# Reordering the first microseconds of a float16 gated MLP: loads, turns, plain columns and one cast

## The chip, the cores and the metric

One Trainium2 chip (trn2), one core of it. The metric is the device time of the program in microseconds (us), the median of several executions. The span of a profile is 1.7 to 1.9 us shorter than that time. A run would count as slow if it were over 1.5% above the fastest of its kernel.

## The reference

```python
# x: (16, 256, 512)   w1: (512, 4096)   w2: (2048, 512), all float32
h = x @ w1
gate, value = np.split(h, 2, axis=-1)
h = np.maximum(gate, 0) * value
return (h @ w2).astype(np.float32)
```

## The kernel before

The kernel rounds to float16 and multiplies 2x2 blocked matrices with Strassen-like schemes of seven products (P1 to P7), so it needs sums and differences of blocks as operands. It works in four stages of 1024 rows each. In a stage, 16 "blocks" of 128 hidden columns give g (first product), and then g times w2 gives the output (second product). In the first stage the operands have to be made while TensorE already wants them: x comes in as float32 and is turned (transposed, 128 columns at a time) by TensorE; the four sums S1 to S4 of x come from VectorE; the four differences T1 to T4 of w1, for each pair of blocks, come from GpSimd; ScalarE casts the parts of w1 that need no difference. To have something to multiply before the sums exist, blocks 0 and 1 are done as "plain" products of eight matmuls per half of the rows. Products land in the tiles X, W and Y (in PSUM, the memory for results); an "eviction" is the instruction of VectorE or ScalarE that reads such a tile out, and the program lets TensorE write the tile again only after it.

```python
    # names of the profile: x_A, x_S = x and its sums; w_B, w_T = w1 and its differences;
    # v_B, v_T = the same of w2; w_stage = where w1 lands, later the sums of g
    fetch(0, nc.scalar)                 # w1 block 0, on ScalarE's queue
    fetch_first(0)                      # x blocks 0..3
    fetch(1, nc.sync)                   # w1 block 1
    make_identity(nc, ident)
    fetch_first(1)                      # x blocks 4..7
    fetch(2, nc.sync)                   # w1 blocks 2 and 3
    fetch(3, nc.sync)                   # w1 blocks 4 and 5
    # ... cut
    rest = plain_w(0)
    turn_first(xo, 0, 0, new_w())       # four float32 turns, two evictions
    keep_busy(2)                        # warm matmuls
    turn_first(xo, 0, 1, new_x())
    rest()
    keep_busy(4)
    turn_first(xo, 0, 2, new_x())
    keep_busy(2)
    turn_first(xo, 0, 3, new_w())
    keep_busy(2)
    plain[0].products(0, *first_half, half)     # gate and value together
    plain_w(1)()
    fetch(4, nc.sync)
    plain[0].products(0, *first_half, other)
    plain[0].value()                    # ScalarE: W out of PSUM
    plain[0].gate(0)                    # VectorE: max(X, 0) * v
    # ... cut: block 1 with the turns of x blocks 4..7 between, then the sums of x
    prepare(2)                          # GpSimd: T1..T4 of blocks 2 and 3, each for both blocks
    copy_some(3)                        # ScalarE: their three casts
    fetch(5, nc.sync)                   # w1 blocks 8 and 9, into the place of 2 and 3
    # ... cut
    prepare(3)

    # in a block of the first product
        def P1(self):
            # ... X <- B11 A11 ; then ScalarE copies X to Y
            nc.scalar.copy(out=self.Y, in_=self.X)

    # first stage, once: GpSimd, the differences of w2
                if (s, n, jb) == (0, "P7", 13):
                    nc.gpsimd.tensor_tensor(vop["T1"], vop["T3"], vop["B11"], op=SUB)
                    nc.gpsimd.tensor_tensor(vop["T2"], vop["B22"], vop["T1"], op=SUB)

    # second product: a "look" squares one operand on ScalarE (a range check), 1.05 us
        def P4(self):
            nc.scalar.activation(self.o[:, 1, :DO // 2], self.Y, COPY, scale=1 / GS)
            self.send(1, slice(0, DO // 2 if self.end else DO))
            if self.t < (2 if self.s else 3):
                some_look()
```

## Time and profile before

| | before |
|---|---|
| median time (first three runs: 310.92 to 311.54) | 311.07 us |
| span in the profile | 309.2 us |
| TensorE busy | 301.5 us (98%) |
| first plain product | 8.68 us |
| P1 of block 2 / P4 of block 2 | 17.39 / 23.30 us |
| last matmul | 304.27 us |

The page's head and its share of each engine:

```profile
span 309.2 us, 5211 instructions
PE 301.5 (98%) x1870; PEld 183.2 (59%) x1870; DVE 236.4 (76%) x378; ACT 177.0 (57%) x350; POOL 153.7 (50%) x186
```

TensorE (PE) is the limit. Whatever it gains must come from places where it waits or does work that counts for nothing, and those lie at the start. The next lines are from the timeline of PE before: start and length in us, engine, line, operation, output and inputs; in brackets the idle time before it and what ended it. One line merges several instructions.

```profile
1.27 3.17 PE L145 MATMUL Y<-warm 128*128 128x512 f16 x7 [1.27 <-DVE warm L141]
4.62 0.63 PE L448 MATMUL W<-ident,x_A 128*128 128x128 f32 x4 [0.18 <-DMA x_A<-in_x_dram]
...
8.68 0.38 PE L301 MATMUL X<-x_A,w_B 128*128 128x256 f16 x2
...
17.39 0.59 PE L233 MATMUL X<-x_A,w_B 128*128 128x512 f16 x2
17.82 0.59 PE L233 MATMUL W<-x_S,w_T 128*128 128x512 f16 x2
18.64 0.59 PE L233 MATMUL X<-x_A,w_B 128*128 128x512 f16 x2 [0.23 <-ACT Y L240]
...
23.30 0.59 PE L233 MATMUL Y<-x_A,w_T 128*128 128x512 f16 x2 [0.47 <-DVE cc L266]
```

The first product that is needed starts at 8.68 us. Block 2 starts at 17.39 us, and P4 of block 2, which needs the last of the differences, at 23.30 us. I use that P4 as a milestone: what comes before it is the start, what comes after is "the body". A pair of 512-column matmuls should follow the one before by 0.43 us, so the start 18.64 after 17.82 hides a stall of 0.39 us, more than the bracket shows, because the length of a matmul is modelled.

GpSimd (POOL) before: its first difference waits for w1 blocks 2 and 3 to land.

```profile
15.57 1.36 POOL L215 TENSOR_TENSOR w_T<-w_stage 128x512 f16<-128x512 f32 x1 [5.44 <-DMA w_stage<-in_w_dram]
...
54.48 1.53 POOL L187 DMA_DIRECT2D x<-in_x_dram  x3
56.01 4.09 POOL L580 TENSOR_TENSOR v_T<-v_T,v_B 128x2048 f16<-128x2048 f16 x1
60.18 4.06 POOL L581 TENSOR_TENSOR v_T<-v_B,v_T 128x2048 f16<-128x2048 f16 x1
```

VectorE (DVE) before, where the sums of g for the second product begin, in the same stretch:

```profile
64.02 0.78 DVE L164 TENSOR_TENSOR w_stage<-g 128x1024 f16<-128x1024 f16 x1
64.88 0.69 DVE L164 TENSOR_TENSOR w_stage<-w_stage,g 128x1024 f16<-128x1024 f16 x1
```

### The profile page before, as it was taken

The numbers are of one execution on the slowest core, as the hardware profiler recorded it, in microseconds if no ns is written. First come the engines' busy times: TensorE is split into PE (matmuls) and PEld (weight loads), VectorE is DVE, ScalarE is ACT, GpSimd is POOL, SyncE is SP. The second block draws the span as 40 slices with busy tenths as digits, with TensorE's granted clock in tenths as the row PEclk, the third lists the DMA queues.
The fourth block names the chain that finished last, engine by engine and source line by source line (L and its number), as shares of the span: only waits on it lengthen the run. The fifth ranks groups of instructions, "written<-read, shape, count | busy, mean of one in ns | idle before, by whom it ended". The sixth has DMA issues, their size and how long they took to land.

```text
span 309.2 us, 5211 instructions
## 1 busy us (share of the span) xinstructions
PE 301.5 (98%) x1870; PEld 183.2 (59%) x1870; DVE 236.4 (76%) x378; ACT 177.0 (57%) x350; POOL 153.7 (50%) x186
## 2 busy tenths in 40 slices
PE   7999999999999999999999999999999999999994
PEld 3844444588854444478864444458884444448883
DVE  1598888889678888887538888888536888888841
ACT  2588886445865555537855555546956555553231
POOL 2199999930048899500028889700006988700000
PEclk9999999999999999999999999999999999999999
DMA  7977696998594233001354400000325110000132
GB/s 236 355 230 251 176 232 87 196 214 149 164 303 101 69 70 68 2 0 47 127 184 105 119 0 4 0 0 15 122 103 171 37 34 1 0 3 0 70 136 72
DMA packets 37340, 32.87 MB, mean 106 GB/s; under 512 B 14400, under 2 KB 32320, under 8 KB 37184
## 3 DMA queue, kind: packets, MB, share of 16 engines
q1 hardware_dynamic: 31904, 25.70, 27.2%
q0 software_dynamic: 4352, 6.29, 11.8%
q10 hardware_dynamic: 1056, 0.52, 0.6%
q8 instruction: 15, 0.25, 0.3%
q14 instruction: 13, 0.11, 0.1%
HBM read 27.26 MB, written 12.58 MB: 129 GB/s over the span
## 4 chain that ended last, share of the span: by engine, by line
PE 93%; DVE 2%; DMA 2%; issue 1%; SPq 0%; ACT 0%; DVEq 0%
PE Y L233 26%; PE X L233 17%; PE W L233 17%; PE Y L333 14%; PE X L333 9%; PE W L333 9%; DMA x_A<-in_x_dram 2%; DVE x_S L164 1%; PE X L448 1%; DVE g L308 1%; PE X L301 1%; PE W L301 1%; PE W L448 0%; PE Y L150 0%; DVE x_S L450 0%
## 5 line engine op out<-in xcount | busy, mean ns | idle before, releaser
L233 PEld LDWEIGHTS <-w_T 128*128 128x128 f16 x496 | 48.5, 98 | 57.5 <-issue 1.0
L170 POOL TENSOR_TENSOR fold<-xh 128x1024 f32<-128x1024 f16 x16 | 30.3, 1894 | 93.1 <-DMA xh<-x 92.1
L233 PE MATMUL X<-x_A,w_B 128*128 128x512 f16 x248 | 73.7, 379 | 0.2 <-ACT Y L240 0.2
L233 PE MATMUL Y<-x_S,w_T 128*128 128x512 f16 x248 | 73.8, 379 | 0.0
L233 PEld LDWEIGHTS <-w_B 128*128 128x128 f16 x372 | 36.4, 98 | 42.6 <-issue 0.8
L240 ACT COPY Y<-X 128x512 f32<-128x512 f32 x62 | 35.4, 570 | 39.8 <-PE X L233 39.5
L260 DVE SCALAR_TENSOR_TENSOR cc<-W,pu 128x512 f32<-128x512 f32 x62 | 42.8, 691 | 19.5 <-ACT pu L254 19.5
L254 ACT ACTIVATE pu<-Y 128x512 f32<-128x512 f32 x62 | 37.0, 597 | 34.1 <-PE Y L233 32.8
L173 POOL TENSOR_TENSOR fold<-fold 128x512 f32<-128x512 f32 (+2 forms) x96 | 51.8, 540 | 7.5
L333 PEld LDWEIGHTS <-w_stage 128*128 128x128 f16 x512 | 50.0, 98 | 6.3 <-issue 0.4
L266 DVE SCALAR_TENSOR_TENSOR cc<-Y,pu 128x512 f32<-128x512 f32 x62 | 42.8, 691 | 7.2 <-PE Y L233 0.7
L261 DVE SCALAR_TENSOR_TENSOR g<-X,cc 128x512 f16<-128x512 f32 x62 | 42.9, 691 | 2.3
L276 DVE SCALAR_TENSOR_TENSOR g<-Y,cc 128x512 f16<-128x512 f32 x62 | 42.2, 681 | 1.8 <-PE Y L233 1.8
L333 PEld LDWEIGHTS <-g 128*128 128x128 f16 x384 | 37.6, 98 | 8.2
L233 PE MATMUL Y<-x_A,w_T 128*128 128x512 f16 x124 | 36.9, 379 | 0.5 <-DVE cc L266 0.5
L247 ACT ACTIVATE pu<-W 128x512 f32<-128x512 f32 x62 | 37.2, 600 | 0.2 <-ACT Y L240 0.2
L233 PE MATMUL W<-x_S,w_T 128*128 128x512 f16 x124 | 36.9, 379 | 0.0
L233 PE MATMUL W<-x_S,w_B 128*128 128x512 f16 x124 | 36.9, 379 | 0.0
L333 PE MATMUL Y<-v_T,w_stage 128*128 128x256 f16 x256 | 33.2, 272 | 0.1
L333 PE MATMUL X<-v_B,g 128*128 128x256 f16 x256 | 31.9, 273 | 0.0
L164 DVE TENSOR_TENSOR w_stage<-g 128x1024 f16<-128x1024 f16 x32 | 21.5, 686 | 0.2
L365 DVE SCALAR_TENSOR_TENSOR o<-W,pu 128x256 f32<-128x256 f32 x16 | 6.7, 422 | 18.7 <-PE W L333 18.7
(84 smaller groups left out, 283.8 us busy)
## 6 DMA issues: line engine op xcount, KB each, us to landing
out_dram<-o SPq DMA_DIRECT2D x30, 256.0 KB, 2.0
w_stage<-in_w_dram SPq DMA_DIRECT2D x14, 512.0 KB, 5.7
x<-in_x_dram POOLq DMA_DIRECT2D x4, 1024.0 KB, 12.9
xh<-x SPq DMA_DIRECT2D x16, 256.0 KB, 3.1
v_B<-in_w_dram POOLq DMA_DIRECT2D x3, 512.0 KB, 6.3
x_S<-in_x_dram SPq DMA_DIRECT2D x4, 256.0 KB, 5.5
x_A<-in_x_dram SPq DMA_DIRECT2D x3, 256.0 KB, 4.9
w_stage<-in_w_dram ACTq DMA_DIRECT2D x2, 256.0 KB, 4.6
```

The lines of the kernel that those rows point to most:

```text
L164: yield eng.tensor_tensor(o[n], o[i0], o[i1], op=op)
L170: nc.gpsimd.tensor_tensor(fold, t, t, op=MULT)
L173: nc.gpsimd.tensor_tensor(fold[:, :, :m], fold[:, :, :m], fold[:, :, m:2 * m], op=ADD)
L233: nc.tensor.matmul(ps, wop[wn][:, b, self.jb * P:(self.jb + 1) * P], self.xo[xn][:, b, :], start=fresh and b == 0, stop=b == 1, skip_group ...
L240: nc.scalar.copy(out=self.Y, in_=self.X)
L247: nc.scalar.activation(self.p5, self.W, COPY, scale=GS)
L254: nc.scalar.activation(self.u2, self.Y, COPY, scale=GS)
L260: nc.vector.scalar_tensor_tensor(out=self.c12, in0=self.W, scalar=GS, in1=self.u2, op0=MULT, op1=ADD)
L261: nc.vector.scalar_tensor_tensor(out=self.g[:, self.jb, :TH], in0=self.X, scalar=0.0, in1=self.c12, op0=MAX, op1=MULT)
L266: nc.vector.scalar_tensor_tensor(out=self.c22, in0=self.Y, scalar=GS, in1=self.p5, op0=MULT, op1=ADD)
L276: nc.vector.scalar_tensor_tensor(out=self.g[:, self.jb, TH:], in0=self.Y, scalar=0.0, in1=self.c22, op0=MAX, op1=MULT)
L333: nc.tensor.matmul(ps, self.op[an][:, i], vop[wn][:, i], start=name in ("P1", "P5") and i == 0, stop=i == NJ // 2 - 1, skip_group_check=True)
```

## The change

The intent: bring the first two x blocks in ahead of everything else, with only the gate half of w1 block 0 between x blocks 1 and 2, so that gate products start earlier; take float16 turns for the second half of x; let the plain products of the first columns go ahead of the last turns; keep TensorE's clock up with warm matmuls where it waits; and move one cast of x, which GpSimd issues, out of the first stage. The differences of blocks 2 and 3 are made one block at a time, the sums of x in halves; the looks and a few VectorE jobs have new places. Cuts are marked with dots; the comments in it and in the code above are mine.

```diff
-    fetch(0, nc.scalar)
-    fetch_first(0)
+    fetch_first(0, (0, 1))
+    ws[0] = load_w1(nc.sync, *wl[0], (0,))
+    fetch_first(0, (2, 3))
+    load_w1(nc.sync, *wl[0], (1,))
     fetch(1, nc.sync)
     make_identity(nc, ident)
-    fetch_first(1)
+    fetch_first(1, range(4))
     ...
-    turn_first(xo, 0, 0, new_w())
-    keep_busy(2)
-    turn_first(xo, 0, 1, new_x())
-    rest()
-    keep_busy(4)
     ...
+    turn_first(xo, 0, 0, halves(*YS), (dve, act))
+    XS = [new_x(), new_x()]
+    turn_first(xo, 0, 1, halves(*XS), (dve, act))
+    arm(YS[0])                       # a 512-column warm matmul; its zeros are used later
+    arm(YS[1])
+    keep_busy(3)
+    plain[0].open(W=False)
+    plain[0].part("gate", *first_half, half)
+    turn_first(xo, 0, 2, halves(*XS), (dve, act))
+    turn_first(xo, 0, 3, halves(new_w(), new_w()), (dve, act))
+    keep_busy(2)
+    plain[0].part("gate", *first_half, other)
     ...
+    cast_first(0, pool)              # float16 casts of x blocks 4..7
+    cast_first(1, dve)
+    cast_first(2, pool)
+    turn_first(xo, 1, 0, (turns(YS[0])[0], turns(YS[1])[0]), (dve, act))
     ...
-    prepare(2)
-    copy_some(3)
-    fetch(5, nc.sync)
+    prepare(2, False)                # differences of blocks 2 and 3, block by block
+    sum_w1(6)
     ...
+    prepare(3, False)
+    w_sums[:4] = [w_sums[i] for i in (2, 0, 3, 1)]   # rest of 2 and 3 mixed with 4 and 5
+    sum_w1()
+
+    def last_plain():                # called after P1 of block 2
+        plain[1].part("value", *second_half, other, False)
+        copy_some(1)
+        fetch(5, nc.sync)
     ...
-            if self.t < (2 if self.s else 3):
+            if self.t in ((0, 2) if self.s else (0, 1, 2)):
                 some_look()
     ...
-            self.end = s == NS - 1 and t == NB // 2 - 1
+            self.end = s == NS - 1 and t != NB // 2 - 2
     ...
-    CASTS = {(0, 11): 1, (0, 13): 0, (0, 14): 2, (1, 8): 3}
+    CASTS = {(0, 11): 1, (0, 14): 2, (1, 8): 3, (2, 3): 0}
-    SUMS_FIRST = (10, 11, 13, 45), (17, 22, 26, 53), (33, 37, 41, 64), (67, 72, 76, 80)
+    SUMS_FIRST = (10, 11, 13, 45), (17, 22, 26, 53), (33, 37, 41, 66), (67, 72, 76, 80)
     ...
-            ... ("T4", "B21", "T2", (57, 58))
+            ... ("T4", "B21", "T2", (57, 64))
```

More of the change, by code (lines that the diff above doesn't have):

```diff
@@ L142, in fast_way @@
     ident = wpool.tile([P, P], F32, name="ident")
+    Y = psy.tile([P, TH], F32, name="Y", tag="Y")
     for i in range(NWARM):
-        Y = psy.tile([P, TH], F32, name="Y", tag="Y")
         nc.tensor.matmul(Y, warm_b[:, :P], warm_b[:, :TH], start=True, stop=True)
@@ L159, in x_tiles, with sum_of @@
         return o
+    SUMS_X = {"S1": ("A21", "A22", ADD), "S2": ("S1", "A11", SUB), "S4": ("A12", "S2", SUB), "S3": ("A11", "A21", SUB)}
+    def sum_of(o, n, eng=nc.vector):
+        i0, i1, op = SUMS_X[n]
+        eng.tensor_tensor(o[n], o[i0], o[i1], op=op)
     def sums_of(o, eng=nc.vector):
-        for n, i0, i1, op in (("S1", "A21", "A22", ADD), ("S2", "S1", "A11", SUB), ("S4", "A12", "S2", SUB),
-                              ("S3", "A11", "A21", SUB)):
-            yield eng.tensor_tensor(o[n], o[i0], o[i1], op=op)
+        for n in SUMS_X:
+            yield sum_of(o, n, eng)
     def look(t, at):
@@ L201, in load_rows, with load_w1, w1_ops, operands @@
         return t
-    def load_w1(eng, jb, n, u):
+    def load_w1(eng, jb, n, u, vs=(0, 1)):
         t = w_stage[:, u:u + n].rearrange("p u v -> p (u v)").rearrange("p (g e j) -> p g e j", g=2, e=4)
-        for v in range(2):
+        for v in vs:
             eng.dma_start(out=t[:, v], in_=w1_v[v, :, :, jb * P:(jb + n) * P])
         return t.rearrange("p g (k b) j -> p k b g j", k=2)
-    def w1_ops(jb, n, t):
-        js = slice(jb * P, (jb + n) * P)
-        b11, b21, b12, b22 = t[:, 0, :, 0], t[:, 1, :, 0], t[:, 0, :, 1], t[:, 1, :, 1]
-        op = {n: w[:, :, js] for n, w in wop.items()}
-        nc.gpsimd.tensor_tensor(op["T1"], b12, b11, op=SUB)
-        nc.gpsimd.tensor_tensor(op["T2"], b22, (op["T1"]), op=SUB)
-        nc.gpsimd.tensor_tensor(op["T3"], b22, b12, op=SUB)
-        nc.gpsimd.tensor_tensor(op["T4"], b21, (op["T2"]), op=SUB)
+    def w1_ops(jb, n, t, m):
+        def operands(j0, m):
+            js = slice((jb + j0) * P, (jb + j0 + m) * P)
+            b11, b21, b12, b22 = (t[:, k, :, v, j0 * P:(j0 + m) * P] for v in range(2) for k in range(2))
+            return {n: w[:, :, js] for n, w in wop.items()}, b11, b21, b12, b22
+        steps = [(0, i, n) for i in range(4)]
+        if m < n:
+            steps = [(j0, i, m) for j0, i in ((0, 0), (0, 1), (m, 0), (0, 2), (m, 1), (0, 3), (m, 2), (m, 3))]
+        def step(j0, i, m):
+            op, b11, b21, b12, b22 = operands(j0, m)
+            nc.gpsimd.tensor_tensor(op[f"T{i + 1}"], (b12, b22, b22, b21)[i], (b11, op["T1"], b12, op["T2"])[i], op=SUB)
+        w_sums.extend(lambda a=a: step(*a) for a in steps)
+        op, b11, b21, b12, b22 = operands(0, n)
         return [lambda o=o, i=i: nc.scalar.copy(out=o, in_=i)
@@ L290, in __init__, with open, part @@
             self.g, self.jb = g, jb
-        def products(self, h, a1, a2, cols=(0, TH)):
+        def open(self, X=None, W=None):
+            self.X = psx.tile([P, TH], F32, name="X", tag="X") if X is None else X
+            self.W = psw.tile([P, TH], F32, name="W", tag="W") if W is None else W
+        def part(self, which, a1, a2, cols=(0, TH), fresh=True):
             js, c = slice(self.jb * P, (self.jb + 1) * P), slice(*cols)
-            if cols[0] == 0:
-                self.X = psx.tile([P, TH], F32, name="X", tag="X")
-                self.W = psw.tile([P, TH], F32, name="W", tag="W")
-            for a, gate, value in ((a1, "B11", "T3"), (a2, "B21", "B22")):
-                for ps, wn in ((self.X, gate), (self.W, value)):
-                    for b in range(2):
-                        nc.tensor.matmul(ps[:, c], wop[wn][:, b, js], a[:, b, c], start=a is a1 and b == 0,
-                                         stop=a is a2 and b == 1)
+            ps, names = (self.X, ("B11", "B21")) if which == "gate" else (self.W, ("T3", "B22"))
+            for a, wn in zip((a1, a2), names):
+                for b in range(2):
+                    nc.tensor.matmul(ps[:, c], wop[wn][:, b, js], a[:, b, c], start=fresh and a is a1 and b == 0,
+                                     stop=a is a2 and b == 1, skip_group_check=not fresh)
         def value(self):
@@ L305, in value, with held @@
             nc.scalar.activation(self.v, self.W, COPY, scale=GS)
+        def held(self, h):
+            X, v = self.X, self.v
+            return lambda: nc.vector.scalar_tensor_tensor(out=self.g[:, self.jb, h * TH:(h + 1) * TH], in0=X, scalar=0.0,
+                                                          in1=v, op0=MAX, op1=MULT)
         def gate(self, h):
-            nc.vector.scalar_tensor_tensor(out=self.g[:, self.jb, h * TH:(h + 1) * TH], in0=self.X, scalar=0.0,
-                                           in1=self.v, op0=MAX, op1=MULT)
+            self.held(h)()
     s_place = w_stage[:, :4].rearrange("p u v -> p (u v)").bitcast(F16).rearrange("p (i n h t) -> p i n h t", i=2, n=4, t=P)
@@ L412, in fetch, with sum_w1, prepare @@
             ws[i] = load_w1(eng, jb, n, u)
-    def prepare(i):
+    w_sums = []
+    def sum_w1(n=None):
+        for job in w_sums[:n]:
+            job()
+        del w_sums[:n]
+    def prepare(i, at_once=True):
         jb, n, _ = wl[i]
-        copies.extend((i, c) for c in w1_ops(jb, n, ws.pop(i)))
+        copies.extend((i, c) for c in w1_ops(jb, n, ws.pop(i), 1 if i == 2 else n))
+        if at_once:
+            sum_w1()
     def copy_some(n):
@@ L440, in fast_way, with fetch_first, cast_first, turn_first @@
     xn = [[t.rearrange("p a b -> p (a b)").bitcast(F32) for t in place[4 * h:4 * h + 4]] for h in range(2)]
-    def fetch_first(h):
-        for b in range(4):
-            nc.sync.dma_start(out=xn[h][b], in_=x_nat[0, h, b])
-    def turn_first(o, h, b, ps):
-        for e in range(4):
-            nc.tensor.transpose(ps[:, e * P:(e + 1) * P], xn[h][b][:, e * P:(e + 1) * P], ident)
-        for k, copy in ((0, nc.vector.tensor_copy), (1, nc.scalar.copy)):
-            copy(out=o[f"A{h + 1}{k + 1}"][:, :, b * P:(b + 1) * P],
-                 in_=ps[:, k * 256:k * 256 + 256].rearrange("p (b t) -> p b t", b=2))
+    x16_first = [halfs.tile([P, 8, P], F16, name="xh", tag="xh").rearrange("p (b q) c -> p b (q c)", b=2) for _ in range(2)]
+    ident16 = wpool.tile([P, P], F16, name="ident16")
+    half, other = (0, TH // 2), (TH // 2, TH)
+    def fetch_first(h, bs):
+        for b in bs:
+            nc.sync.dma_start(out=xn[h][b], in_=x_nat[0, h, b])
+    def cast_first(b, copy):
+        copy(out=x16_first[b // 2][:, b % 2], in_=xn[1][b])
+    def turn_first(o, h, b, places, copies):
+        rows, one = (x16_first[b // 2][:, b % 2], ident16) if h else (xn[0][b], ident)
+        for k in range(2):
+            for e in range(2):
+                nc.tensor.transpose(places[k][:, e * P:(e + 1) * P],
+                                    rows[:, (2 * k + e) * P:(2 * k + e + 1) * P], one)
+        for k in range(2):
+            copies[k](out=o[f"A{h + 1}{k + 1}"][:, :, b * P:(b + 1) * P],
+                      in_=places[k].rearrange("p (b t) -> p b t", b=2))
     def new_x():
@@ L457, in new_w, with new_y, arm @@
         return psw.tile([P, TH], F32, name="W", tag="W")
-    fetch(0, nc.scalar)
-    fetch_first(0)
+    def new_y():
+        return psy.tile([P, TH], F32, name="Y", tag="Y")
+    def arm(ps):
+        nc.tensor.matmul(ps, warm_b[:, :P], warm_b[:, :TH], start=True, stop=True)
+    dve, act, pool = nc.vector.tensor_copy, nc.scalar.copy, nc.gpsimd.tensor_copy
+    fetch_first(0, (0, 1))
+    ws[0] = load_w1(nc.sync, *wl[0], (0,))
+    fetch_first(0, (2, 3))
+    load_w1(nc.sync, *wl[0], (1,))
     fetch(1, nc.sync)
     make_identity(nc, ident)
-    fetch_first(1)
+    fetch_first(1, range(4))
     fetch(2, nc.sync)
     fetch(3, nc.sync)
+    dve(out=ident16, in_=ident)
     xo = x_tiles()
@@ L468, in fast_way, with halves, turns @@
     first_half, second_half = (xo["A11"], xo["A12"]), (xo["A21"], xo["A22"])
-    half, other = (0, TH // 2), (TH // 2, TH)
-    rest = plain_w(0)
-    turn_first(xo, 0, 0, new_w())
+    YS = [new_y(), new_y()]
+    def halves(*ts):
+        return [t[:, :2 * P] for t in ts]
+    def turns(t):
+        return [t.bitcast(F16)[:, c:c + 2 * P] for c in (0, 2 * P)]
+    rest = plain_w(0)
+    turn_first(xo, 0, 0, halves(*YS), (dve, act))
+    XS = [new_x(), new_x()]
+    turn_first(xo, 0, 1, halves(*XS), (dve, act))
@@ L472, in fast_way @@
+    arm(YS[0])
[5 more added lines that the diff above has]
+    turn_first(xo, 0, 3, halves(new_w(), new_w()), (dve, act))
     keep_busy(2)
-    turn_first(xo, 0, 1, new_x())
+    plain[0].part("gate", *first_half, other)
+    plain[0].W = new_w()
     rest()
-    keep_busy(4)
-    turn_first(xo, 0, 2, new_x())
-    keep_busy(2)
-    turn_first(xo, 0, 3, new_w())
-    keep_busy(2)
@@ L480, in fast_way @@
-    plain[0].products(0, *first_half, half)
-    plain_w(1)()
-    fetch(4, nc.sync)
-    plain[0].products(0, *first_half, other)
-    plain[0].value()
-    plain[0].gate(0)
-    plain[1].products(0, *first_half, half)
-    ps = [new_x(), new_w()]
-    for b in range(4):
-        turn_first(xo, 1, b, ps[b % 2])
-        if b == 1:
-            plain[1].products(0, *first_half, other)
-            plain[1].value()
-    plain[1].gate(0)
-    sums = sums_of(xo)
-    prepare(2)
-    copy_some(3)
-    fetch(5, nc.sync)
@@ L498, in fast_way @@
-    next(sums)
-    plain[0].products(1, *second_half, half)
-    next(sums)
-    next(sums)
-    plain[0].products(1, *second_half, other)
-    plain[0].value()
-    plain[0].gate(1)
-    prepare(3)
-    plain[1].products(1, *second_half)
+    rest = plain_w(1)
+    plain[0].part("value", *first_half)
+    plain[0].value()
+    plain[1].open()
+    plain[1].part("gate", *first_half)
+    rest()
+    fetch(4, nc.sync)
+    plain[0].gate(0)
+    plain[1].part("value", *first_half)
+    spare = plain[0].X, plain[1].W
@@ new lines, in fast_way @@
+    cast_first(0, pool)
+    cast_first(1, dve)
+    cast_first(2, pool)
+    turn_first(xo, 1, 0, (turns(YS[0])[0], turns(YS[1])[0]), (dve, act))
+    turn_first(xo, 1, 1, (turns(plain[0].X)[0], turns(plain[0].W)[0]), (dve, act))
+    plain[1].value()
+    held = plain[1].held(0)
+    cast_first(3, dve)
+    xo["S3"] = halfs.tile([P, 8, P], F16, name="xh", tag="xh").rearrange("p (a b) c -> p a (b c)", a=2)
+    sums = [sums_of({n: t[:, :, slice(*c)] for n, t in xo.items()}) for c in (half, other)]
@@ new lines, in fast_way @@
+    next(sums[0])
+    plain[0].open()
+    plain[0].part("gate", *second_half, half)
+    turn_first(xo, 1, 2, turns(spare[0]), (act, act))
+    turn_first(xo, 1, 3, turns(spare[1]), (dve, dve))
+    plain[0].part("value", *second_half, half)
+    plain[1].open(*reversed(YS))
+    plain[1].part("gate", *second_half, half)
+    plain[1].part("value", *second_half, half)
+    next(sums[1])
+    next(sums[0])
+    next(sums[1])
+    plain[0].part("gate", *second_half, other)
+    plain[0].part("value", *second_half, other)
@@ new lines, in fast_way, with last_plain_out @@
+    for n in ("S4", "S3"):
+        sum_of(xo, n)
+    held()
+    prepare(2, False)
+    sum_w1(6)
+    copy_some(1)
+    plain[0].value()
+    copy_some(1)
+    plain[1].part("gate", *second_half, other, False)
+    prepare(3, False)
+    w_sums[:4] = [w_sums[i] for i in (2, 0, 3, 1)]
+    sum_w1()
+    def last_plain():
+        plain[1].part("value", *second_half, other, False)
+        copy_some(1)
+        fetch(5, nc.sync)
+    def last_plain_out():
+        plain[1].value()
+        plain[0].gate(1)
+        plain[1].gate(1)
@@ L544, in fast_way @@
     for n, at in enumerate(ats):
-        LOOKX[at] = n // 4, n % 4
+        LOOKX[at] = (n // 4 + 1) % NS, n % 4
     rows = []
@@ L595, in fast_way @@
                 if s == 0 and (n, jb) == ("P1", NPLAIN):
-                    plain[1].value()
+                    last_plain()
                 if s == 0 and (n, jb) == ("P5", NPLAIN):
-                    next(sums)
-                    plain[1].gate(1)
-                if n in ("P6", "P7"):
+                    last_plain_out()
+                if n == "P7" or (n, jb) == ("P5", NPLAIN + 1) or n == "P6" and (s, jb) != (0, NPLAIN):
                     copy_some(1)
@@ L619, in fast_way @@
         if s == 0:
-            for n2, i0, i1, at in (("T3", "B22", "T3", (46, 50)), ("T4", "B21", "T2", (57, 58))):
+            for n2, i0, i1, at in (("T3", "B22", "T3", (46, 50)), ("T4", "B21", "T2", (57, 64))):
                 for i, u in enumerate(at):
```

## The prediction

> **What bounds the kernel now.** TensorE. The page gives PE 301.5 us busy of a span of 309.2 us at a granted clock of 0.999; the table by stretches shows it 99.97 of 100 us busy from 100 to 200 us, and as full elsewhere from 24 us to 304.5 us. Nothing in the diff removes matmuls from that body. The change can win only in the first 24 us and in the 4.6 us after the last matmul.
>
> **The start, from the timeline of TensorE.** First x block 4.62 us, first plain product 8.68, plain products end and block 2 begins (P1) 17.39, its P5 17.82, its P4 23.30; no gap after that. Pitches: 0.215 us per 512-column matmul, 0.109 per float32 128-column turn. Needed work up to 17.39 is 8 x 0.436 + 32 x 0.215 = 10.4 us, so 7.0 us are start, warming and waiting. From 17.39 to 23.30 another 1.2 us are lost: 0.39 before P2 (ScalarE's copy of X), 0.15 before P3, 0.64 before P4 (VectorE). VectorE is solid from 14.5 to 24 us.
>
> **What the change does.**
> - w1 block 0 moves to the x queue, its gate half between x blocks 1 and 2. Bytes are the same. DMA moves about 350 GB/s without a break from 3 to 20 us, so x blocks 0 and 1 land earlier (estimate 3.8 and 4.5 us), but w1 blocks 2 and 3 stay at about 15.5 us.
> - Gate products of block 0 start near 6.3 us in place of 8.68; then the last x block (11.5 to 12 us) and w1 block 1 (9 us) limit. My walk through the order ends the plain work, one value part left over, near 16.2 us.
> - Float16 turns: I assume half of 0.436 us, saving up to 0.9 us, against two added 512-column warm matmuls (0.43 us) and five fewer 256-column ones (0.54 us). Four added casts use GpSimd and VectorE while they have room.
> - GpSimd's first subtraction takes one block (estimate 0.7 us) in place of two (1.36 us); T4 of block 2 comes 2 us earlier. S1 and S2 run in halves before GpSimd starts. Trainium skill, "SBUF — State Buffer", the section on the two sides of the memory: a VectorE instruction with two SBUF inputs and a GpSimd one that reads SBUF exclude each other. This trace agrees: sums of x take 1.16 to 1.64 us beside GpSimd, 0.68 alone.
> - The cast of x moved to a later stage, the rotated looks, the split outputs of the last stage: off the critical path, 0 to 0.2 us.
>
> **Critical path.** P5 of block 2 near 17.0 in place of 17.82 (0.8 us), and of the 1.2 us of stalls 0.9 goes, as P1 no longer waits behind value copies, the plain gates come later and the sums earlier. P4 of block 2 near 21.6 in place of 23.30. Gain 1.7 us at the start plus 0.1 at the end: 309.2 us, range 308.1 to 310.4. Over 2% faster needs 6.2 us, most of the start's waste, with the same bytes to bring: 0.02. Slower by 2% has no mechanism I see: 0.01. Within 2%: 0.97.
>
> **What would show it.** First plain matmul near 6.3 us; last float16 turns near 13.5; P5 of block 2 near 17; its P4 at 21 to 22; GpSimd's first subtraction still at 15.5; the span after that P4 unchanged (285.9 us) within 0.3.
>
> **What would make it wrong.** Float16 turns as slow as float32; one queue starting slower than two; casts on GpSimd and VectorE excluding each other; VectorE's backlog (4 x 0.69 us per 3.02 us block) passing the stall to a later block; or later w1 loads becoming the limit.

## The result and the profile after

| | before | after |
|---|---|---|
| median time, four runs each | 311.09 us (310.92 to 311.54) | 310.19 us (309.94 to 310.39) |
| ratio | 1 | 0.9969, 95% interval 0.9951 to 0.9986 |
| span in the profile | 309.2 | 308.2 |
| P4 of block 2 | 23.30 | 21.79 |
| last matmul | 304.27 | 303.23 |
| body: last matmul less P4 of block 2 | 280.97 | 281.44 |

A ratio is the mean time of one kernel's fast runs over the mean of the other's in the same rounds, so it is not quite the ratio of the medians. The change saves 0.9 us, or 0.3%: within 2%, inside the range that was given, and half of the 1.9 us that the middle of it promised.

The head of the page after, and lines from PE's timeline:

```profile
span 308.2 us, 5215 instructions
PE 301.5 (98%) x1863; PEld 182.4 (59%) x1863; DVE 235.8 (77%) x383; ACT 176.7 (57%) x350; POOL 154.7 (50%) x192
```

```profile
1.28 3.17 PE L145 MATMUL Y<-warm 128*128 128x512 f16 x7 [1.28 <-DVE warm L141]
4.24 1.06 PE L485 MATMUL Y<-ident,x_A 128*128 128x128 f32 x4
...
6.96 0.60 PE L314 MATMUL X<-x_A,w_B 128*128 128x256 f16 x4
...
11.75 0.39 PE L485 MATMUL Y<-ident,xh 128*128 128x128 f16 x4
11.97 0.28 PE L485 MATMUL X<-ident,xh 128*128 128x128 f16 x2
...
16.21 0.59 PE L245 MATMUL X<-x_A,w_B 128*128 128x512 f16 x2
...
17.08 0.60 PE L245 MATMUL W<-x_S,w_T 128*128 128x512 f16 x2
17.62 0.59 PE L245 MATMUL X<-x_A,w_B 128*128 128x512 f16 x2
...
21.79 0.59 PE L245 MATMUL Y<-x_A,w_T 128*128 128x512 f16 x2
...
29.98 0.59 PE L245 MATMUL X<-x_A,w_B 128*128 128x512 f16 x2 [0.26 <-ACT Y L252]
```

The start went much as planned. Gate products begin at 6.96 us, P1 of block 2 at 16.21, its P5 at 17.08, its P4 at 21.79: 1.51 us earlier. Four float16 turns take 0.22 us (11.75 to 11.97), half of what float32 ones take. But at 29.98 us there is a new stall, and it is not the only one. I listed each place where a matmul starts more than 0.045 us later than the pitch of the one before allows, from P4 of block 2 to the range check's own small product at about 289 us, which is the same in both kernels:

| stall at | before | after |
|---|---|---|
| 30.0 us, waits for ScalarE's copy of X | none | 0.42 |
| 64.4 us, waits for VectorE's sum of g | none | 0.24 |
| 75.9 and 76.8 us, waits for VectorE's sum of g | none | 0.14 + 0.05 |
| 150.5 and 223.5 us | 0.20 + 0.20 | none |
| sum | 0.40 | 0.85 |

The body is longer by 0.85 - 0.40 = 0.45 us; measured, 0.47. So of 1.51 us won at the start, 0.85 was given back, and 0.40 came from a part of the change that I had put down as costing and saving next to nothing.

GpSimd after, to set against the lines of before:

```profile
15.86 1.01 POOL L227 TENSOR_TENSOR w_T<-w_stage 128x256 f16<-128x256 f32 x1 [3.17 <-DMA w_stage<-in_w_dram]
16.95 1.00 POOL L227 TENSOR_TENSOR w_T<-w_stage,w_T 128x256 f16<-128x256 f32 x1
...
54.49 1.03 POOL L192 DMA_DIRECT2D x<-in_x_dram  x2
55.54 4.08 POOL L670 TENSOR_TENSOR v_T<-v_T,v_B 128x2048 f16<-128x2048 f16 x1
59.70 4.06 POOL L671 TENSOR_TENSOR v_T<-v_B,v_T 128x2048 f16<-128x2048 f16 x1
```

It issues the casts of x at 54.49 us after and 54.48 before: GpSimd has been working without a pause since its data landed, and TensorE's lead of 1.5 us does not move it at all. Only the cast that left the stage (one of three) brings its end forward, by 0.48 us. VectorE after, in the same stretch:

```profile
62.93 1.38 DVE L165 TENSOR_TENSOR w_stage<-g 128x1024 f16<-128x1024 f16 x1
64.41 0.69 DVE L165 TENSOR_TENSOR w_stage<-w_stage,g 128x1024 f16<-128x1024 f16 x1
```

and TensorE's weight loads (PEld), which wait for that first sum:

```profile
64.37 0.77 PEld L351 LDWEIGHTS <-w_stage 128*128 128x128 f16 x8 [0.36 <-DVE w_stage L165]
```

The first sum of g now starts at 62.93 us, while GpSimd's last difference still runs to 63.76, and it takes 1.38 us in place of 0.69. The Trainium skill, page "SBUF — State Buffer", the section on the two sides of the memory, says that a VectorE instruction with two SBUF inputs and a GpSimd one that reads SBUF hold an exclusive lock against each other. This trace agrees: the sum ends 0.55 us after GpSimd does, and so it is in every profile below in which VectorE gets to that sum before one long GpSimd instruction ends, wherever that end lies. Before, VectorE came to that sum only 0.22 us ahead of GpSimd's end, and nobody noticed.

ScalarE after, around the stall at 30 us:

```profile
27.60 0.60 ACT L266 ACTIVATE pu<-Y 128x512 f32<-128x512 f32 x1
28.83 0.62 ACT L231 CAST w_B<-w_stage 128x512 f16<-128x512 f32 x1 [0.63 <-DMA w_stage<-in_w_dram]
29.35 0.58 ACT L252 COPY Y<-X 128x512 f32<-128x512 f32 x1
```

ScalarE works in order. A cast of w1 blocks 8 and 9 waits for its load, and the copy of X that P2 of block 6 needs stands behind it. The load is late because its place is freed late: GpSimd's last difference of blocks 2 and 3 has been mixed with those of blocks 4 and 5. Before, that load was issued at 21.77 us; after, at 24.29.

The stalls at 150 and 223 us that went away: ScalarE before,

```profile
149.02 1.05 ACT L179 ACTIVATE sq<-w_T 128x1024 f16<-128x1024 f16 x1
149.97 0.19 ACT L179 ACTIVATION_READ_ACCUMULATOR sq<-w_T 128x1 f32 x1
150.06 0.37 ACT L360 ACTIVATE pu<-Y 128x256 f32<-128x256 f32 x1
```

and after:

```profile
148.97 0.38 ACT L378 ACTIVATE pu<-Y 128x256 f32<-128x256 f32 x1 [0.49 <-PE Y L351]
149.25 1.05 ACT L184 ACTIVATE sq<-w_T 128x1024 f16<-128x1024 f16 x1
150.19 0.19 ACT L184 ACTIVATION_READ_ACCUMULATOR sq<-w_T 128x1 f32 x1
```

The look, 1.05 us of squaring, used to stand ahead of the eviction of Y that P7 waits for. Now the eviction goes first.

### The profile page after: what moved, and what is told of

It is laid out like the page before. It is cut to its first block, busy times and chain, and to the rows that moved or that the text cites. A ratio compares the mean times of both kernels' runs of the same rounds, so it can differ in the third digit from the quotient of the medians.

```text
span 308.2 us, 5215 instructions
## 1 busy us (share of the span) xinstructions
PE 301.5 (98%) x1863; PEld 182.4 (59%) x1863; DVE 235.8 (77%) x383; ACT 176.7 (57%) x350; POOL 154.7 (50%) x192
## 4 chain that ended last, share of the span: by engine, by line
PE 97%; DVE 1%; ACT 0%; issue 0%; DVEq 0%
PE Y L245 26%; PE X L245 17%; PE W L245 17%; PE Y L351 14%; PE W L351 9%; PE X L351 8%; PE Y L145 1%; PE X L314 1%; PE W L314 1%; PE Y L314 1%; DVE w_stage L165 0%; PE X L485 0%; PE Y L485 0%; DVE x_A L488 0%; DVE g L288 0%; PE Y L502 0%
## 5 line engine op out<-in xcount | busy, mean ns | idle before, releaser
L245 PE MATMUL Y<-x_S,w_T 128*128 128x512 f16 x220 | 65.5, 379 | 0.0
```

What stands on the lines that cost most here:

```text
L245: nc.tensor.matmul(ps, wop[wn][:, b, self.jb * P:(self.jb + 1) * P], self.xo[xn][:, b, :], start=fresh and b == 0, stop=b == 1, skip_group ...
```

## The experiments

All kernels gave correct results. There were twelve runs in four sets; the sets ran on different chips, but each set ran beside the kernel before on its own chip. The table has what the timed runs and one profile of each say. All twelve kernels are within 2% of the kernel before, and the 95% interval of a ratio reaches 0.0015 to 0.003 to each side, so by time alone most of them can't be told apart.

| run | median us (range) | before, same set | ratio | first subtraction | P4 of block 2 | body | stalls in the body, us |
|---|---|---|---|---|---|---|---|
| after_again | 310.01 (309.76 to 310.37) | 311.36 | 0.9958 | 16.19 | 21.97 | 281.45 | 30: 0.29, 65: 0.39, 76: 0.19 |
| pool_f2_first | 310.61 (310.40 to 310.93) | 311.36 | 0.9975 | 16.71 | 22.50 | 281.59 | 24: 0.54, 65: 0.25, 77: 0.19 |
| looks_back | 311.01 (310.57 to 311.42) | 311.36 | 0.9985 | 16.68 | 22.46 | 281.85 | 31: 0.34, 65: 0.35, 77: 0.19, 150 and 223: 0.40 |
| turns_f32 | 310.74 (310.37 to 311.68) | 311.36 | 0.9976 | 15.87 | 24.54 | 280.77 | 78: 0.19 |
| skip_copy | 310.34 (310.01 to 310.80) | 311.16 | 0.9963 | 16.58 | 22.38 | 281.45 | 65: 0.68, 77: 0.19 |
| v_split | 310.46 (309.79 to 311.31) | 311.16 | 0.9966 | 16.64 | 22.43 | 281.41 | 30: 0.24, 75 to 77: 0.57 |
| w1_actq | 310.23 (309.95 to 312.61) | 311.16 | 0.9973 | 15.48 | 25.15 | 280.77 | 79: 0.19 |
| cast_back | 311.33 (310.73 to 312.30) | 311.16 | 1.0004 | 15.78 | 21.79 | 282.43 | 30: 0.20, 65: 1.02, 76: 0.19, 86: 0.44 |
| skip_cast | 310.24 (309.51 to 310.80) | 311.31 | 0.9959 | 16.41 | 22.18 | 281.64 | 64: 0.18, 76: 0.19, 85: 0.69 |
| sums_back | 310.22 (310.06 to 310.64) | 311.31 | 0.9963 | 16.60 | 22.37 | 281.25 | 30: 0.15, 65: 0.51 |
| no_keep_busy | 310.23 (309.80 to 311.05) | 311.31 | 0.9962 | 16.49 | 22.26 | 281.44 | 30: 0.26, 65: 0.41, 76: 0.19 |
| three_moves | 310.99 (310.29 to 311.44) | 311.43 | 0.9982 | 17.40 | 23.21 | 281.51 | 65: 0.18, 86: 0.74 |

"First subtraction" is the start of GpSimd's first difference, which ends a wait for w1 blocks 2 and 3, so it tells when they landed. How to read this table: kernels that begin with the same instructions (all but turns_f32, w1_actq and no_keep_busy) still got that load at moments from 15.78 to 17.40 us, and their P4 followed it. A difference of half a microsecond between two medians may therefore be the start's luck. For edits that only touch the time after 24 us I take the verdict from the body and the stalls, and use the medians as a check.

### The changed kernel again

The reference of the first set, with no edit.

> The changed kernel once more, as the reference of this call. Theory A (the gain is the start's 1.5 us less what is given back later): 309.9 to 310.5 us, and the stalls of TensorE at about 30.0 us (0.42), 64.4 (0.24) and 75.9 us (0.14) come back in the profile. Theory B (half clock): the changed kernel's first profile showed the full TensorE clock only from 6.45 us, the kernel before from 4.56 us; if that is the phase of the run and not the change, this profile may show another moment, and the start of block 2 may move with it by up to 0.4 us.

The stalls came back at the same places (0.29, 0.39, 0.14 and 0.05 us), the body to 0.01 us, and the gain in time was 1.35 us of medians (ratio 0.9958). The full TensorE clock came at 5.09 us in this profile, 1.36 us earlier than in the first; yet P4 of block 2 came 0.18 us later, with the load 0.33 us later. So an earlier full clock did not bring an earlier start here. It is not ruled out everywhere: in the two profiles with the earliest load on one queue and float16 turns (15.86 us in the changed kernel's first, 15.78 in cast_back, both with the full clock from 6.45 us), P4 came at 21.79 us in both, so something other than the load set it.

### GpSimd's order: the load that is late

```diff
-    w_sums[:4] = [w_sums[i] for i in (2, 0, 3, 1)]
```

> GpSimd's rest of blocks 2 and 3 goes before the subtractions of blocks 4 and 5, so their place is free earlier and the next load is issued near 22.8 us in place of 24.3. Theory A (the wait at 30 us is this late load, which blocks ScalarE's copies in order): the stall of 0.42 us at 30 us is gone. If nothing behind it limits, the time is 309.8 (0.4 less). Rival A2 (GpSimd's fixed chain to 64 us limits the end of the first stage): the stall at 30 goes but the one near 63 to 64 us grows by about as much, since TensorE arrives 0.4 us earlier and GpSimd does not, and the time stays within 0.1 us of the changed kernel.

The stall at 30 us is gone, so the late load was its cause. But a stall of 0.54 us appeared at 23.90 us, ended by GpSimd (PE's timeline of this run):

```profile
22.93 0.59 PE L245 MATMUL X<-x_A,w_B 128*128 128x512 f16 x2
23.90 0.60 PE L245 MATMUL W<-x_S,w_T 128*128 128x512 f16 x2 [0.38 <-POOL w_T L227]
```

T1 of block 4 comes too late when the rest of blocks 2 and 3 goes first. The mixed order was needed for that. The body is 0.14 us longer than in after_again; the rest of the 0.6 us between the medians is not the edit's to claim, as the load landed 0.52 us later. Neither theory had named this place, and the stall near 65 us did not grow as the rival said (0.25 us): the lead had been lost at 24 us. The rival's reason, that GpSimd is the limit, was right, 40 us ahead of where I looked for it.

### The place of one look

```diff
-            if self.t in ((0, 2) if self.s else (0, 1, 2)):
+            if self.t < (2 if self.s else 3):
```

> Only the place of one look in the second products is put back as before. Theory A: the two gaps of TensorE of 0.2 us each near 150 and 223 us come back, as ScalarE squares 1.05 us ahead of the eviction that frees Y: 310.6 (0.4 slower than the changed kernel). Rival (looks are free, as the prediction said): within 0.1 us.

The gaps at 150.5 and 223.5 us are back, 0.20 us each, and the body is 0.40 us longer than in after_again. The rival is out. The median is 1.0 us longer, more than the edit explains; the profile shows the rest before P4 of block 2 (0.49 us), where the edit changes nothing and the load landed 0.49 us later.

### Float32 turns

```diff
-        rows, one = (x16_first[b // 2][:, b % 2], ident16) if h else (xn[0][b], ident)
+        rows, one = xn[h][b], ident
-        return [t.bitcast(F16)[:, c:c + 2 * P] for c in (0, 2 * P)]
+        return [t[:, c:c + 2 * P] for c in (0, 2 * P)]
-    cast_first(...)          # all four
```

> The turns of the second half of x in float32, without the four casts. The prediction's step: 16 turns cost 0.054 us more each on TensorE, 0.9 us in all, of which most counts if TensorE is the limit from 11.7 us on: 310.9 (0.7 slower). Rival (the landing of x and of w1 blocks 2 and 3, not TensorE, sets the start): the casts' own time goes too, x blocks turn as soon as they land, and the time is within 0.2 us of the changed kernel.

0.73 us slower in the median than after_again, near the 0.7 that was expected. That fits the prediction's step but does not show its size: in the same set pool_f2_first and looks_back started 0.5 us later than after_again with no edit of the start, and the casts went together with the turns. Its profile fell on the slowest of the six runs (311.68 us), with the full clock only from 7.32 us, and shows P4 of block 2 at 24.54; it is not a fair picture of the five others. Even so it carries a lesson: that start is 2.57 us later than in after_again, the end only 1.88 us. When TensorE arrives late, the stalls at 30 and 65 us are not there.

### ScalarE's cast put off

```diff
-                if n == "P7" or (n, jb) == ("P5", NPLAIN + 1) or n == "P6" and (s, jb) != (0, NPLAIN):
+                if n == "P7" or (n, jb) == ("P5", NPLAIN + 1) or n == "P6" and (s, jb) not in ((0, NPLAIN), (0, 5)):
```

> The changed kernel with ScalarE's first copy of w1 blocks 8 and 9 put off by one place, so that it does not wait for the late load in front of block 6's copy of X. Theory A: the stall at 30 us (0.29 to 0.42) is gone, and with it 0.3 to 0.4 us: 309.7. Rival A2 (GpSimd's chain ends at 63.8 us whatever TensorE does): VectorE's first sum of the second product starts 0.3 to 0.4 us earlier, waits that much longer for GpSimd, the stall near 64.2 us grows from 0.24-0.39 to 0.6-0.75, and the last matmul and the time stay where they are within 0.1 us.

This is the experiment that tells the two theories apart, and the rival won. The stall at 30 us is gone; the stall at 65 us is 0.68 us in place of 0.39; the body is 281.45 us, as in after_again. VectorE of this run:

```profile
63.09 1.82 DVE L165 TENSOR_TENSOR w_stage<-g 128x1024 f16<-128x1024 f16 x1
65.00 0.69 DVE L165 TENSOR_TENSOR w_stage<-w_stage,g 128x1024 f16<-128x1024 f16 x1
```

The sum takes 1.82 us and ends at 64.91, 0.55 us after GpSimd's last difference (64.36). The stalls up to 65 us add up to 0.66, 0.68, 0.68, 0.66 and 0.67 us in the changed kernel's first profile, after_again, skip_copy, sums_back and no_keep_busy, however they are split between 30 and 65. GpSimd's chain ends 47.7 to 47.9 us after its data landed in all five. TensorE cannot get past that; a stall taken out ahead of it is paid there. The other runs bear this out. GpSimd's end less P4 of block 2 is 41.97 to 41.99 us in these five, 41.49 in skip_cast and three_moves (stalls up to 65 us: 0.18), 42.53 in cast_back (1.22) and 40.94 in the kernel before (none): in every profile but v_split's, the stalls up to 65 us are that distance less 41.3 us, to 0.02 us, and none where it is shorter.

### GpSimd's long instructions cut up

```diff
-                    nc.gpsimd.tensor_tensor(vop["T1"], vop["T3"], vop["B11"], op=SUB)
-                    nc.gpsimd.tensor_tensor(vop["T2"], vop["B22"], vop["T1"], op=SUB)
+                    for n2, i0, i1 in (("T1", "T3", "B11"), ("T2", "B22", "T1")):
+                        for c in range(0, NJ // 2, NJ // 8):
+                            part = [vop[n3][:, c:c + NJ // 8] for n3 in (n2, i0, i1)]
+                            nc.gpsimd.tensor_tensor(*part, op=SUB)
```

> The changed kernel with GpSimd's two subtractions of w2 (4.06 us each) cut into four pieces each, so that VectorE's sum waits for about 1 us at most. If the stall near 64.4 us is VectorE shut out by one long GpSimd instruction, it shrinks to near 0 and the time by 0.25 to 0.35 us: 309.7. Rival: GpSimd's pieces cost more than the whole, its end moves later than 63.8 us, and the wait comes back at the sums that need its result: no gain, stalls between 64 and 77 us at least as large as now (0.43 in sum).

The rival again. The stall at 64 us is gone, since VectorE's sum now gets in between two pieces, but GpSimd's chain ends 48.90 us after the landing, 1.1 us later than whole. Most of that is the cutting itself: seven of the eight pieces take 1.14 to 1.16 us and follow one another by 1.11 us with no sum between them, where a quarter of the whole is 1.02 us. Only the last piece, beside VectorE's sums, takes longer (1.59 us). Stalls of 0.18, 0.17, 0.17 and 0.05 us near 75 to 77 us take the place of the one at 64; the body is 281.41 us.

### w1 block 0 on the other queue

```diff
-    fetch_first(0, (0, 1))
-    ws[0] = load_w1(nc.sync, *wl[0], (0,))
-    fetch_first(0, (2, 3))
-    load_w1(nc.sync, *wl[0], (1,))
+    fetch(0, nc.scalar)
+    fetch_first(0, range(4))
```

> The changed kernel with w1 block 0 loaded by ScalarE's queue, beside the x blocks, as before. The change's intent says this order makes x blocks 0 and 1 and the gate half late: gate products start near 8.5 us in place of 7.0. Theory D (the landing of w1 blocks 2 and 3 sets the moment of block 2, since its P4 came 5.8 to 5.9 us after GpSimd's first subtraction in all four profiles with float16 turns): a start with two queues brings the same bytes as early or earlier, GpSimd's first subtraction at 15.5 to 15.9, and the time is within 0.2 us of the changed kernel or better. Rival (the first products' place counts): slower by 0.5 us or more, and P4 of block 2 over 6.4 us after the first subtraction.

Four of the six runs took 309.95 to 310.29 us, as the changed kernel does: the order of the first loads, which gives the change its name, is worth nothing in the usual run that these runs can show. The rival is out for those four; their own start was not profiled. The first subtraction came at 15.48 us, near the 15.57 of the kernel before, which also uses two queues. The other two runs took 312.30 and 312.61 us, and the profile fell on the first of them. Its PE timeline:

```profile
1.27 3.17 PE L145 MATMUL Y<-warm 128*128 128x512 f16 x7 [1.27 <-DVE warm L141]
4.65 1.09 PE L485 MATMUL Y<-ident,x_A 128*128 128x128 f32 x4 [0.20 <-DMA x_A<-in_x_dram]
6.27 1.12 PE L485 MATMUL X<-ident,x_A 128*128 128x128 f32 x4 [0.54 <-DMA x_A<-in_x_dram]
...
10.38 0.64 PE L485 MATMUL W<-ident,x_S 128*128 128x128 f32 x4
```

Here turns take twice their time (1.06 to 1.12 us for four, not 0.60 to 0.63) until 10.46 us, from where the record has the full clock, and P4 of block 2 comes at 25.15 us. x blocks arrive late and TensorE idles for 0.2 and 0.5 us in its warm-up. The Trainium skill, page "TensorE: Matmul & The Clock Gate", Part 1, says that the full clock is granted after a window of about 3.4 us of sustained work that runs free of the program; an idle gap in the wrong window would then cost a whole one. The trace fits that, but I did not vary the gap alone, so it is a reading and not shown. The kernel before has the same gaps (0.18 and 0.78 us before its first two turns), and 5 of its 50 runs here took over 312.5 us; none of the changed kernel's ten did. Ten are few, but the record has more: of all 70 runs of kernels with the first loads on one queue (the changed kernel and the ten others of the table) none was more than 1.2 us (a mark set after the times were seen) above its kernel's median in its set, and of the 56 with two queues (the kernel before and this one) 7 were. That speaks for the new load order as a guard against long runs; which part of it guards is not shown, since this edit changes the queue and the order together.

### The cast back in the first stage

```diff
-    CASTS = {(0, 11): 1, (0, 14): 2, (1, 8): 3, (2, 3): 0}
+    CASTS = {(0, 11): 1, (0, 13): 0, (0, 14): 2, (1, 8): 3}
```

> The changed kernel with the cast of the first quarter of x back in the first stage on GpSimd's queue. GpSimd is busy without a break from about 16 to 64 us, so its 0.5 us there move the end of its w2 subtractions from 63.8 to 64.3, VectorE's first sum waits that much longer, and TensorE's stall near 64.4 grows by 0.5: slower by 0.4 to 0.5 us, 310.5. Rival (off the critical path, as the prediction said): within 0.1.

The direction is right, the size was too small. The stall at 65 us is 1.02 us, and a second one of 0.44 us appears at 86 us; the body is 282.43 us, 0.98 us longer than in after_again, and the median is level with the kernel before. The second stall belongs to the next stage's x: while it is being loaded, the third cast still moves its data (GpSimd's DMA queue moved 2.62 MB from 60 to 90 us, 1.57 in the changed kernel), the sums of x start at 83.54 us in place of 81.83, and output combinations on VectorE stand behind them. So taking this one cast out is worth 1 us once TensorE starts early: without it, the early start would have bought nothing.

### Another cast out of the chain, with ScalarE's cast put off

```diff
     # and the edit of skip_copy
-    CASTS = {(0, 11): 1, (0, 14): 2, (1, 8): 3, (2, 3): 0}
+    CASTS = {(0, 11): 1, (0, 15): 2, (1, 8): 3, (2, 3): 0}
```

> The changed kernel with two things: ScalarE's copy put off as in the run that did that alone, and one more cast of x (0.5 us of GpSimd) moved behind GpSimd's w2 subtractions, out of its unbroken chain. Theory (GpSimd's chain is what the gain runs into): its end comes 0.5 us earlier, no stall at 30 us, the stall near 64 to 65 us is 0.2 us or less in place of 0.68 with the copy alone, and the span after P4 of block 2 is 4.6 to 4.9 less than with it: in numbers, last matmul less P4 280.9 to 281.0 us in place of 281.45; time 0.5 us under the changed kernel, 309.6. Rival: a new wait takes it back, last matmul less P4 281.3 or more.

The first half of the theory holds: GpSimd's chain ends 47.26 us after the landing, 0.5 us earlier than in skip_copy, and the stall at 64 us falls from 0.68 to 0.18 us. The second half fails. A stall of 0.69 us at 85 us takes all of it back; the body is 281.64 us. PE and VectorE of this run, then VectorE of the changed kernel's first profile:

```profile
85.27 0.60 PE L351 MATMUL Y<-v_T,g 128*128 128x256 f16 x4 [0.53 <-DVE o L388]
```

```profile
83.14 1.42 DVE L165 TENSOR_TENSOR x_S<-x_S,x_A 128x1024 f16<-128x1024 f16 x2 [3.01 <-issue]
84.47 0.42 DVE L383 SCALAR_TENSOR_TENSOR o<-W,pu 128x256 f32<-128x256 f32 x1
84.81 0.41 DVE L388 SCALAR_TENSOR_TENSOR o<-Y,pu 128x256 f32<-128x256 f32 x1
```

```profile
81.83 1.42 DVE L165 TENSOR_TENSOR x_S<-x_S,x_A 128x1024 f16<-128x1024 f16 x2 [1.60 <-issue]
83.18 0.42 DVE L383 SCALAR_TENSOR_TENSOR o<-W,pu 128x256 f32<-128x256 f32 x1
```

The cast (issued at 63.61 us, landed 9.2 us later) now moves its 1 MB just when the next stage's x is loaded. The sums of x start 1.31 us later, and the combination that frees Y for TensorE is behind them in VectorE's order.

### VectorE's jobs at their old places

```diff
-    SUMS_FIRST = (10, 11, 13, 45), (17, 22, 26, 53), (33, 37, 41, 66), (67, 72, 76, 80)
+    SUMS_FIRST = (10, 11, 13, 45), (17, 22, 26, 53), (33, 37, 41, 64), (67, 72, 76, 80)
-            ... ("T4", "B21", "T2", (57, 64))
+            ... ("T4", "B21", "T2", (57, 58))
```

> The changed kernel with VectorE's second half of T4 of w2 and one sum of g at their places of before. If the moved place of T4 makes the stalls of 0.14 and 0.05 near 76 and 77 us, they go and last matmul less P4 is 281.25 in place of 281.44; the time falls by 0.2 us at most, within the noise. Rival: the moves were there to help against the stall near 64 us, and undoing them makes that one larger by 0.1 or more.

The stalls at 76 and 77 us go, and the body is 281.25 us, as expected. The stalls up to 65 us stay 0.66 us in sum, so the moves were no help there. It is the shortest body of all kernels with the early start and float16 turns whose start did not come late; in time it cannot be told from the changed kernel (ratio 0.9963 to before).

### No warm matmuls in the waits

```diff
-    keep_busy(3)
-    keep_busy(2)
```

> The changed kernel without the five 256-column warm matmuls in the waits at the start (the two wide ones stay, as the sums need the zeros they write). Theory E (the load of w1 blocks 2 and 3 sets the start, the TensorE clock only if it comes very late): the fast runs stay within 0.2 us of the changed kernel and P4 of block 2 is still 5.8 to 5.9 us after GpSimd's first subtraction, but the full clock may come later and one or more of the six runs may be 1 us or more longer, as two of six were with the load on ScalarE's queue (its profile: full clock only from 10.46 us, P4 9.67 us after the subtraction). Rival: warm matmuls cost time on TensorE, and leaving them out gains 0.2 us or more.

310.23 us, P4 of block 2 5.77 us after the first subtraction, body 281.44 us: no difference that these runs show. The full clock came at 4.45 us in its profile. One of six runs took 311.05 us. These five warm matmuls neither cost nor bring anything measurable.

### Three moves together

```diff
     # the edits of skip_copy and sums_back, and
-    CASTS = {(0, 11): 1, (0, 14): 2, (1, 8): 3, (2, 3): 0}
+    CASTS = {(0, 11): 1, (1, 0): 2, (1, 8): 3, (2, 3): 0}
-                if n == "P1" and jb == (14 if s == 0 else 2) and s + 1 < NS:
+                if n == "P1" and jb == (14, 4, 2, 2)[s] and s + 1 < NS:
```

> The changed kernel with ScalarE's copy put off, VectorE's T4 and sum back at their places of before, and the cast of the third quarter of x moved into the second stage, with its loads two blocks later, so that it is in the way neither of GpSimd's chain nor of the loads of the second quarter. Theory: no stall at 30 us, 0.1 to 0.3 us near 64 us, none at 76 us and none near 85 us (which took back 0.69 when the cast was only put behind the w2 subtractions); last matmul less P4 of block 2 280.7 to 280.9 in place of 281.45, time 309.5 to 309.7. Rival: the moved cast and loads meet the second stage's loads and outputs and a stall of 0.3 us or more appears between 84 and 125 us; no gain over the changed kernel.

A miss, and of my own making. The stalls at 30 and 76 us are gone and the one at 65 us is 0.18, but 0.74 us appears at 86 us. The trace of GpSimd shows why: the cast, which I had put at the head of the second stage in program order, was issued at 64.64 us, right behind the w2 differences. A queue issues an instruction when its own waits are done, and this one had none; between the two places in the program GpSimd had nothing to do. So it met the same loads as in skip_cast. No version I tried beats the changed kernel beyond doubt.

## Why the prediction was right or wrong

The class and the range were right; of the 1.9 us in the middle, about half came. Point by point:

- **The start.** "P4 of block 2 near 21.6 in place of 23.30": 21.79 and 21.97 in the two profiles of the changed kernel. The size was right, to 0.2 to 0.4 us, and so were its two parts: P5 "near 17.0" came at 17.08, and from there to P4 it is 4.71 us in place of 5.48, so 0.77 us of stalls went where 0.9 were promised. Gate products "near 6.3" came at 6.96. In this profile the first eight turns ran at the half clock until 6.45 us; but v_split, at full clock from 4.02 us, had them at 7.16, behind a gate half of w1 that landed at 6.65 in place of 5.28 us. Float16 turns take half the time (0.22 us for four, 0.44 in float32); what that is worth, 0.73 us in the medians of turns_f32, may hold some of the start's luck. Which edits bring the 1.51 us is not shown: no run put back GpSimd's pairs of blocks, the whole sums of x or the order of the plain columns alone.
- **"w1 blocks 2 and 3 stay at about 15.5 us": wrong in the mean.** 15.86 in the first profile, 16.19 in the second, and up to 17.40 in kernels that begin the same. In nine of the eleven profiles with float16 turns and w1 on the x queue, that P4 comes 5.77 to 5.81 us after the first subtraction: there the start is this landing plus a constant (5.94 and 6.01 us in the two with the earliest load). Before, that distance is 7.73 us, so the change is worth 1.8 to 1.9 us against the load, and loses some of it to a later load. Both profiles with two queues had it at 15.5 to 15.6. The step that failed is "DMA moves about 350 GB/s without a break": from 4 to 8 us it moved 350 and 352 GB/s in the two profiles with two queues, and 257 to 318 in the twelve with one; from 8 to 15 us it was 350 to 358 in all fourteen. So the lateness of w1 blocks 2 and 3 is made in the first 8 us, before their own turn. I had named "one queue starting slower than two" as a thing to go wrong and put no time on it. Two profiles against twelve, with queue and order changed together, do not settle that the queue is the cause.
- **"The span after that P4 unchanged (285.9 us) within 0.3": this step failed.** It was 286.36 us, 308.15 less 21.79. I treated the body as a block that shifts to the left as a whole. It does not: GpSimd's chain is tied to its load, not to TensorE, and ends at 63.8 us. TensorE's lead of 1.5 us ran into it: 0.66 us of stalls at 30 and 64 us, then 0.19 us by VectorE's new order. skip_copy shows that the 0.66 us is one budget. The prediction listed "later w1 loads becoming the limit" as a risk, and that occurred at 30 us; "VectorE's backlog" names the right engine for 64 us, but what held VectorE there was GpSimd. The term in the sum was zero where 0.85 us was measured.
- **"The cast of x moved to a later stage, the rotated looks, the split outputs of the last stage: off the critical path, 0 to 0.2 us": wrong.** The looks' place was worth 0.40 us (looks_back), and the cast 0.98 us of the body once the start is early (cast_back). The split outputs no run isolates: from the last matmul to the end it is 4.89 us before and 4.92 after, but 4.65 in after_again, which is the same kernel. Nor did a run undo the rotation of the looks at x, another line of the diff.
- **Sum.** 1.51 (start) - 0.85 (given back) + 0.40 (looks) = 1.06 us; the profiles differ by 1.0 us, the first four timed runs by 0.9, the later six by 1.35. That the result lies well inside the range is partly luck: a loss of 0.85 us and a gain of 0.40 us, both put at next to nothing, have opposite signs.

What stays open: why DMA with one queue is slower from 4 to 8 us, and by amounts that differ, so that the same load lands at moments 1.6 us apart in programs with the same first instructions, and what makes long runs rarer with the changed loads.

## What to carry to other kernels

When a limit is lifted at the start of a pipeline, ask which engine's timetable does not move with it. Here GpSimd was busy without a pause for 48 us behind one load, and the stage could end no sooner than its chain did; a stall taken out ahead of such a chain comes back at its end, with the same sum. And an engine that works in order makes cheap jobs costly by their place: a cast waiting for a load, or a range check ahead of an eviction, each held TensorE for 0.15 to 0.42 us, while in a queue the place in the program is no date at all.

## What the Trainium skill lacked or had wrong

- "TensorE: Matmul & The Clock Gate", Part 1: "The transition happens around 4µs into sustained matmul activity, ±500ns run-to-run." Here the first matmul ran at 1.27 to 1.28 us in all fourteen profiles, and the full clock was recorded from 4.02 to 7.32 us of the span, once from 10.46 us: 2.7 to 6.1 us after the first matmul, and 9.2 in the run with idle gaps. The spread, 3.3 us without that run, is about three times what the page gives, and the page does not say what a short idle gap in the first windows costs.
- "Trainium Kernel Development and Optimization", Key Constraints, says that issuing DMAs from several engines only saves the sequencer's issue time. In the two profiles with the first loads on two queues, w1 blocks 2 and 3 had landed by 15.48 and 15.57 us; in twelve with the same bytes on one queue at 15.78 to 17.40 us, after a slower stretch from 4 to 8 us (257 to 318 GB/s, not 350). That is too little to contradict the page, and no page says how much the landing of one and the same load order varies.
- "SBUF — State Buffer" has the lock between VectorE and GpSimd, and the runs agree (a sum of g took up to 2.17 us in place of 0.69, ending 0.55 us after GpSimd's instruction).
- No page gives the price of cutting up a GpSimd instruction so that VectorE gets in between: a difference of 4.06 to 4.09 us took 4.48 us in four pieces with no sum of VectorE's beside them.
